# Seven products instead of eight for three pairs of groups in the first feed-forward layer, and sums and remainders of a pair's weights as operations of 2048 columns

## The chip, the cores and the metric

The kernel runs on one core of one Trainium2 chip. The metric is device time in microseconds (us) of one launch. Of the kernel before, three timed runs gave a median of 937.63 us (936.35 to 939.73); one further execution was recorded by the profiler, and every duration below comes from that one.

Five engines work side by side, each through its own list of instructions in order: PE (matrix products into PSUM), DVE (element by element), ACT (functions and copies), POOL (here a few small operations), SP (issues the loads). They wait for each other through semaphores.

## The reference, cut to what matters

The trunk has two layers on 256 tokens of 1024 features. Each layer adds half a SwiGLU feed-forward net, then a mixer (attention and pooling in layer 0, a state-space layer in layer 1), then another half SwiGLU net. So there are four nets, numbered f = 0 to 3 here, each with its own weights and D_FF = 2816.

```python
def _swiglu(h, w_gate, w_up, w_down):
    return (jax.nn.silu(h @ w_gate) * (h @ w_up)) @ w_down

x = x + 0.5 * _swiglu(_rmsnorm(x, ffn_norm[layer, 0]), ffn_w_gate[layer, 0], ...)
```

All is float32. Net 0 is the first work of the kernel: it runs while the machine starts up.

## The kernel before, in words

**Products in float32.** Each operand of a matrix product is split into a high part and a remainder, both in a reduced float32 type, and a product is three matmuls: high by high, remainder of the weights by high, high by remainder of the activations. ACT makes the high part (`wh`, L184), DVE the remainder (`wl`, L141 as `tt`). The activations h, transposed, lie in `hTh` and `hTl`.

**Groups.** D_FF is cut into NG = 11 groups of 256 columns, numbered 0 to 10. A group's gate and up weights are two units (`f` units, halves of the 1024 rows; 4096 columns of a partition together), its down weights one unit (2048 columns). PE computes gate and up for both halves of the tokens (t = 0, 1): 4 blocks of 12 matmuls of 512 columns into PSUM tiles `wk`; ACT applies silu (`sg`), DVE multiplies (`pr`); PE transposes the result (`sk<-ident,pr`), ACT and DVE split it (`hh`, `hl`); then 24 matmuls of the *previous or same* group's down projection into the accumulators `acc`. `ffn_joint` writes that order.

**Pairs.** In net f = 3 three pairs of groups, beginning at 2, 5 and 8 (PAIRS, L43), use another formula: the gate/up product of two groups is a 2 by 2 block product (two halves of the 1024 input features by two groups, two halves of the tokens), and in Strassen's form, as Winograd wrote it, it takes 7 block products instead of 8, each of 12 matmuls of 512 columns (`pair_product`, j = 1 to 7, in the order 1, previous down, 6, 2, 7, 5, 4, 3). For that it needs sums of weights: `split_pair` makes them on DVE, three for j = 6 and one for j = 7, then splits each operand (`m` units; their raw data are the `sr` tiles, four of 1 MB). It also needs sums of activations (`pair_rows`, on DVE) and their transposes `sTh`, `sTl` (`pair_turn`, four times four transposes on PE, put behind the blocks of group 1). The sums of products are made by DVE (one by ACT) out of PSUM into tiles `u`: `u1` from j = 6, `u0` from j = 2 and so on; `u0` to `u3` feed `gate`, whose product is named `pp`. Two `wk` tiles exist, so the product after next can start only when the sums have read a `wk` tile.

**Order.** A list of steps is written out (`S(...)`). Before each step `pump` issues loads and splits ahead as far as the ring of split buffers (RING = 4 units) and of raw buffers (RAW = 4 pieces of 512 KB) allow. Each engine's list follows from these steps with priorities; PE, DVE and ACT keep their order at run time. A buffer of the split ring becomes free when PE has finished the product four units earlier; so the copy for j = 4 waits for the end of product 6, and that for j = 3 for the end of product 2.

**Net 0** starts with `first`, `second`, `third` (loading and transposing x), then groups 0 to 10 jointly. After group 3 `opened` loads the mixer's constants and issues the rotary tables, some sixty small operations on DVE, in between. `tail` ends it.

Of the kernel before, what the change touches and what calls it, by code (L numbers as in the profile page):

```python
# [42 lines left out]
PAIRS = {3: (2, 5, 8)}  # L43
# [69 lines left out]
def trunk_kernel(ctx: ExitStack, tc: tile.TileContext, I, out):  # L113
# [199 lines left out]
    def split_pair(u):  # L313

        _, f, g, j = u
        b11, b21, b12, b22 = (raws.get((f, g, n, kh)) for n in range(2) for kh in range(2))
        h, l = (wsp.tile([128, 4, 2, 256], F32R, tag=tg, name=tg) for tg in ("wh", "wl"))
        lf = pr_["t2"]
        parts = [slice(0, 2), slice(2, 4)]
        with behind("split"):  # L320
            if j == 6:
                for k in parts:
                    tt(b11[:, k], b12[:, k], b11[:, k], ALU.subtract)
                    tt(lf[:, k], b11[:, k], b22[:, k], ALU.subtract)
                    tt(b21[:, k], b21[:, k], lf[:, k], ALU.add)
            if j == 7:
                for k in parts:
                    tt(b12[:, k], b22[:, k], b12[:, k], ALU.subtract)
            r = {1: b11, 2: b21, 3: b22, 4: b21, 5: b11, 6: lf, 7: b12}[j]
            for k in parts:  # L330
                keep("splits", hi_of(h[:, k], r[:, k]), tt(l[:, k], r[:, k], h[:, k].bitcast(F32), ALU.subtract))
        held[u] = (h, l)
# [122 lines left out]
    def gate_up(f, g, t, kh, ks):  # L455
# [3 lines left out]
        if (f, g, t) not in gups:  # L459
            gups[f, g, t] = wk((128, 2, 256))  # L460
# [32 lines left out]
    def pair_rows(f):  # L493

        a11, a12, a21, a22 = (hn[t][:, c * 512:(c + 1) * 512] for t in range(2) for c in range(2))
        rho = pr_["rho"]
        if f == 0:
            gv = pr_["pool"].tile([128, DM], F32, name="pg")
            SP.dma_start(out=gv, in_=I["ffn_norm"][0, 0].partition_broadcast(128))
            for t in range(2):  # L500
                for c in range(2):
                    o = slice(c * 512, (c + 1) * 512)
                    tt(hn[t][:, o], xs[t][:, o], gv[:, o], ALU.mult)
        root = pr_["pool"].tile([128, 1], F32, name="root")
# [56 lines left out]
    def hid_T(f, g, *ts):  # L561
# [6 lines left out]
        ps = sk((128, 2, len(ts) * 128))  # L568
# [22 lines left out]
    def even_open():  # L591
        at["pool"] = p = tc.alloc_tile_pool(name="even", bufs=1)
# [6 lines left out]
        at["psc"] = p.tile([128, 4], F32, name="psc")  # L599
# [5 lines left out]
        SP.dma_start(out=at["pos"], in_=I["positions"][0].rearrange("(t p) -> p t", p=128))  # L605
        at["qk"] = [p.tile([128, 2, 8, 64], F32, name=f"qk{t}") for t in range(2)]
# [16 lines left out]
        at["cs"] = p.tile([128, 2, 2, 2, 8], F32, name="cs")  # L623
# [94 lines left out]
    def rotary_tables():  # L718
        p = at["pool"]
# [699 lines left out]
    def ffn_joint(f, g0, g1):  # L1419

        for g in range(g0, g1):
            paced.add(len(steps))
            for kh in range(2):
                if f == 1 and g == NG - 1 and kh:
                    S(hold)
                for t in range(2):
# [3 lines left out]
                    if g == 1 and f in PAIRS:  # L1430
                        S(lambda n=2 * kh + t: pair_turn(n))
# [5 lines left out]
    def ffn_pairs(f, g0, g1):  # L1437

        g = g0
        while g < g1:  # L1440
# [10 lines left out]
            HID(f, g, 0, 1)  # L1451
            dn(f, g, 0)
# [60 lines left out]
    def first():  # L1513
        row = hn[1][0:8, 0:128]
# [60 lines left out]
    ffn_joint(0, 1, 4)  # L1575

    def opened():
        with behind("load"):
            load_g("m0", I["mix_norm"][0])
            even_open()  # L1580
        rotary_tables()
    S(opened)
    ffn_joint(0, 4, NG)
# [43 lines left out]
    S(lambda: at["pool"].release())  # L1627
# [147 lines left out]
```

## Time and profile before

| | |
|---|---|
| median of 3 runs | 937.63 us (936.35 to 939.73) |
| profiled execution | 937.66 us, span 935.9 us |
| PE busy | 914.7 us (98%) |
| DVE busy | 711.3 us (76%) |
| ACT busy | 464.9 us (50%) |
| loads and stores | 184.59 MB, mean 197 GB/s |

The span runs from the first to the last instruction recorded; the profiled execution's own time is 1.76 us longer. A row of a timeline gives start, duration, engine, line of the program, operation and operands; "x4" is four instructions merged, so the distance of two starts, not the duration, is what a block costs. In brackets stands the idle time before and what ended it. Net 0 takes the span's first 199 us, net 3 the last 175 us.

### The profile page before, as it was taken

What the parts mean: (1) busy time and instruction counts of PE and PEld (TensorE: products, weight loads), DVE (VectorE), ACT (ScalarE), POOL (GpSimd) and SP (SyncE); (2) the same over time, 40 slices, a digit from 0 to 9 for tenths busy, and PEclk for the clock granted to TensorE, in tenths of its full rate; (3) what the DMA queues carried; (4) which work ended last, traced back from release to release, by engine and by line L of the source; (5) the groups of instructions that cost most, each with busy time, mean ns of one, the idle gap of its engine ahead of it and who ended that gap; (6) DMA issues with size and microseconds to landing.
All of it is one profiled execution on the core that took longest, in us unless ns stands there. A gap on an engine that the chain in (4) does not pass through costs nothing.

```text
span 935.9 us, 13253 instructions
## 1 busy us (share of the span) xinstructions
PE 914.7 (98%) x4981; PEld 755.9 (81%) x4981; DVE 711.3 (76%) x1141; ACT 464.9 (50%) x643; POOL 64.9 (7%) x114
## 2 busy tenths in 40 slices
PE   7999999999999999999999999999879999999998
PEld 5888888889988888888888888888658788887876
DVE  5756654578967659999896557999496689999992
ACT  6544444455536444434454444444345465656561
POOL 0000000013020000000132001600200000000000
PEclk9999999999999999999999999999999999999999
DMA  7867656654476877556788655865956941939141
GB/s 249 276 193 219 192 183 200 193 166 142 134 193 202 197 228 209 174 154 209 235 240 295 191 180 165 250 206 183 301 217 194 333 148 47 335 101 320 53 134 46
DMA packets 149055, 184.59 MB, mean 197 GB/s; under 512 B 23160, under 2 KB 131648, under 8 KB 148224
## 3 DMA queue, kind: packets, MB, share of 16 engines
q1 hardware_dynamic: 145184, 174.70, 60.0%
q0 software_dynamic: 3504, 8.92, 3.8%
q8 instruction: 39, 0.64, 0.3%
q10 hardware_dynamic: 304, 0.14, 0.1%
q14 instruction: 24, 0.20, 0.1%
HBM read 173.24 MB, written 9.44 MB: 195 GB/s over the span
## 4 chain that ended last, share of the span: by engine, by line
PE 76%; DVE 9%; DMA 7%; ACT 3%; issue 3%; POOL 1%; SPq 0%; ACTq 0%; DVEq 0%; POOLq 0%
PE wk L103 46%; PE acc L103 25%; PE sk L103 5%; DMA raw<-in_ffn_w_up_dram 3%; DVE wl L141 3%; DMA raw<-in_s_w_glu_dram 2%; ACT wh L184 1%; DMA V<-x 1%; DVE X L141 1%; DVE b_t L141 1%; POOL r L742 1%; DMA raw<-in_ffn_w_gate_dram 1%; ACT acc L383 0%; ACT h L1211 0%; DVE b_q L141 0%
## 5 line engine op out<-in xcount | busy, mean ns | idle before, releaser
L141 DVE TENSOR_TENSOR wl<-raw,wh 128x1024 fp32r<-128x1024 f32 (+1 forms) x281 | 335.1, 1217 | 119.6 <-ACT wh L184 118.7
L184 ACT ACTIVATE wh<-raw 128x1024 fp32r<-128x1024 f32 (+1 forms) x281 | 285.6, 1051 | 216.0 <-PE wk L103 94.5
L103 PE MATMUL wk<-wh,hTh 128*128 128x512 f32 (+1 forms) x776 | 203.1, 380 | 3.0 <-DVE pr L150 1.5
L103 PE MATMUL wk<-wl,hTh 128*128 128x512 f32 (+1 forms) x776 | 200.2, 377 | 0.0
L103 PE MATMUL wk<-wh,hTl 128*128 128x512 f32 (+1 forms) x776 | 199.4, 376 | 0.0
L103 PEld LDWEIGHTS wk<-wh,hTh 128*128 128x128 f32 x776 | 139.6, 189 | 30.2 <-ACT hTh L184 2.5
L103 PEld LDWEIGHTS wk<-wl,hTh 128*128 128x128 f32 x776 | 140.8, 189 | 26.5 <-DVE wl L141 0.2
L103 PEld LDWEIGHTS wk<-wh,hTl 128*128 128x128 f32 x776 | 140.8, 189 | 26.4
L103 PE MATMUL acc<-wh,hh 128*128 128x512 f32 x352 | 141.4, 402 | 1.4 <-ACT hh L184 1.4
L103 PE MATMUL acc<-wl,hh 128*128 128x512 f32 x352 | 137.2, 390 | 0.0
L103 PE MATMUL acc<-wh,hl 128*128 128x512 f32 x352 | 137.0, 392 | 0.0
L478 ACT ACTIVATE sg<-wk,rstd 128x256 f32<-128x256 f32 x76 | 35.8, 472 | 95.1 <-PE wk L103 90.5
L103 PEld LDWEIGHTS acc<-wh,hh 128*128 128x128 f32 x352 | 66.2, 188 | 14.8 <-ACT hh L184 2.7
L103 PEld LDWEIGHTS acc<-wh,hl 128*128 128x128 f32 x352 | 66.1, 188 | 14.8 <-DVE hl L141 0.7
L103 PEld LDWEIGHTS acc<-wl,hh 128*128 128x128 f32 x352 | 66.3, 188 | 12.4
L150 DVE SCALAR_TENSOR_TENSOR pr<-wk,rstd,sg 128x256 f32<-128x256 f32 x76 | 36.4, 480 | 35.9 <-ACT sg L478 35.9
L141 DVE TENSOR_TENSOR wl<-sr,wh 128x1024 fp32r<-128x1024 f32 x36 | 42.8, 1219 | 2.6 <-ACT wh L184 2.6
L184 ACT ACTIVATE hh<-sk 128x512 fp32r<-128x512 f32 (+1 forms) x52 | 27.4, 527 | 29.6 <-PE sk L103 29.6
L184 ACT ACTIVATE wh<-sr 128x1024 fp32r<-128x1024 f32 x36 | 36.2, 1052 | 11.5 <-PE acc L103 5.2
L141 DVE TENSOR_TENSOR hl<-sk,hh 128x512 fp32r<-128x512 f32 (+1 forms) x52 | 31.3, 604 | 4.3 <-ACT hh L184 4.3
L383 ACT ACTIVATE acc<-x 128x512 f32<-128x512 f32 x24 | 14.3, 597 | 22.6 <-DVE x L150 18.3
L103 PE MATMUL sk<-ident,pr 128*128 128x128 f32 x152 | 24.4, 273 | 0.3 <-DVE pr L150 0.3
(322 smaller groups left out, 819.7 us busy)
## 6 DMA issues: line engine op xcount, KB each, us to landing
raw<-in_ffn_w_down_dram SPq DMA_DIRECT2D x88, 512.0 KB
raw<-in_ffn_w_up_dram SPq DMA_DIRECT2D x76, 512.0 KB
raw<-in_ffn_w_gate_dram SPq DMA_DIRECT2D x75, 512.0 KB
raw<-in_ev_w_in_dram SPq DMA_DIRECT2D x16, 512.0 KB
raw<-in_s_w_glu_dram SPq DMA_DIRECT2D x16, 512.0 KB
sr<-in_ffn_w_gate_dram SPq DMA_DIRECT2D x12, 512.0 KB
sr<-in_ffn_w_up_dram SPq DMA_DIRECT2D x12, 512.0 KB
raw<-in_ev_w_out_dram SPq DMA_DIRECT2D x8, 512.0 KB
```

The lines of the kernel that those rows point to most:

```text
L103: i = f(*a, **k)
L141: return DVE.tensor_tensor(out=o, in0=a, in1=b, op=op)
L150: return DVE.scalar_tensor_tensor(out=o, in0=a, scalar=s, in1=b, op0=op0, op1=op1)
L184: return ACT.activation(out=o, in_=i, func=AF.Copy)
L383: keep("square", ACT.activation(out=into or acc_of(t)[c], in_=xs[t][:, s], func=AF.Square, scale=1.0 / 32.0, accum_out=sums[t][:, c:c + 1]))
L478: ACT.activation(out=sg, in_=ps[:, 0], func=AF.Silu, scale=rstds[f, t])
L742: POOL.tensor_tensor(out=r8, in0=s8, in1=mhalf.to_broadcast([128, 8]), op=ALU.pow)
```

## The change

Net 0 gets three pairs too, beginning at groups 3, 6 and 9, so groups 3 to 10 without 5 and 8 go two by two. With it come the same side works as in net 3: the transposes `pair_turn` (behind the blocks of group 2, since the first pair begins at 3), `pair_rows`, which in net 0 also multiplies x by the norm's gains, loaded once more across all partitions (0.5 MB). The pool of the pair's tiles is open from the start, so the mixer's big tiles are allocated after net 0, its constants before. Group 1's gate and up blocks write to `sk` tiles, group 0's transposes to `wk` tiles. The rotary tables are issued after the first pair. The last pair ends net 0, directly before `tail`.

In both nets the sums and the remainders of `m` units are one operation of 2048 columns where they were two of 1024; the high copies on ACT stay two of 1024.

```diff
-PAIRS = {3: (2, 5, 8)}
+PAIRS = {0: (3,6,9,), 3: (2,5,8,)}
...
         lf = pr_["t2"]
-        parts = [slice(0, 2), slice(2, 4)]
         with behind("split"):
             if j == 6:
-                for k in parts:
-                    tt(b11[:, k], b12[:, k], b11[:, k], ALU.subtract)
-                    tt(lf[:, k], b11[:, k], b22[:, k], ALU.subtract)
-                    tt(b21[:, k], b21[:, k], lf[:, k], ALU.add)
+                tt(b11, b12, b11, ALU.subtract)
+                tt(lf, b11, b22, ALU.subtract)
+                tt(b21, b21, lf, ALU.add)
             if j == 7:
-                for k in parts:
-                    tt(b12[:, k], b22[:, k], b12[:, k], ALU.subtract)
+                tt(b12, b22, b12, ALU.subtract)
             r = {1: b11, 2: b21, 3: b22, 4: b21, 5: b11, 6: lf, 7: b12}[j]
-            for k in parts:
-                keep("splits", hi_of(h[:, k], r[:, k]), tt(l[:, k], r[:, k], h[:, k].bitcast(F32), ALU.subtract))
+            for k in (slice(0, 2), slice(2, 4)):
+                i = hi_of(h[:, k], r[:, k])
+            keep("splits", i, tt(l, r, h.bitcast(F32), ALU.subtract))
...
-            gups[f, g, t] = wk((128, 2, 256))
+
+            gups[f, g, t] = (sk if (f, g) == (0, 1) else wk)((128, 2, 256))
...
         if f == 0:
-            gv = pr_["pool"].tile([128, DM], F32, name="pg")
+            gv = tmp.tile([128, DM], F32, tag="gvec", name="gvec", bufs=1)
             SP.dma_start(out=gv, in_=I["ffn_norm"][0, 0].partition_broadcast(128))
...
-        ps = sk((128, 2, len(ts) * 128))
+        ps = (wk if (f, g) == (0, 0) else sk)((128, 2, len(ts) * 128))
...
-                    if g == 1 and f in PAIRS:
+                    if f in PAIRS and g == PAIRS[f][0] - 1:
                         S(lambda n=2 * kh + t: pair_turn(n))
...
             HID(f, g, 0, 1)
+            if g == NG - 2:
+                return
             dn(f, g, 0)
...
     def first():
+        at["pre"] = tc.alloc_tile_pool(name="even_pre", bufs=1)
+        pair_open(0)
...
-    ffn_joint(0, 1, 4)
+    S(lambda: pair_rows(0))
+    ffn_pairs(0, 1, 5)
 
     def opened():
         with behind("load"):
             load_g("m0", I["mix_norm"][0])
-            even_open()
+            even_load()
         rotary_tables()
     S(opened)
-    ffn_joint(0, 4, NG)
+    ffn_pairs(0, 5, NG)
+    S(lambda: pr_["pool"].release())
+    S(even_open)
     tail(0, N(0, "m0"), HT(0))
```

Three places show what moves. The first is DVE at the start of net 0, from the mean squares (`ss`) to the first `pr` of group 0. Before:

```order
L150 SCALAR_TENSOR_TENSOR ss<-ss 128x1 x2
L141 TENSOR_TENSOR wl<-raw,wh 128x4x256
L150 SCALAR_TENSOR_TENSOR pr<-wk,rstd,sg 128x256
L141 TENSOR_TENSOR wl<-raw,wh 128x4x256
L150 SCALAR_TENSOR_TENSOR pr<-wk,rstd,sg 128x256
```

and now:

```order
L150 SCALAR_TENSOR_TENSOR ss<-ss 128x1 x2
L141 TENSOR_TENSOR prho<-rstd,root 128x1
L141 TENSOR_TENSOR prho<-prho,root 128x1
L141 TENSOR_TENSOR h_85<-x_81,gvec 128x512
L141 TENSOR_TENSOR wl<-raw,wh 128x4x256
L150 SCALAR_TENSOR_TENSOR pr<-wk,rstd,sg 128x256 x2
```

The ratio of the two halves' norms (`prho`, from POOL's `root`) and the first of the four multiplications by the gains now stand ahead of the remainder of the second half of group 1's first unit.

The second place is DVE in the first pair of net 3, from the remainder of j = 6 (`wl<-t`) on; `u_6844` (now `u_6932`) is `u0`, the tile of product 2, `u_6845` (`u_6933`) is `u1`, that of product 6. Before:

```order
L141 TENSOR_TENSOR wl<-t_6848,wh 128x1024
L141 TENSOR_TENSOR sr<-sr 128x1024
L141 TENSOR_TENSOR wl<-sr,wh 128x1024 x2
L141 TENSOR_TENSOR u_6845<-wk,u_6844 128x512
L141 TENSOR_TENSOR wl<-sr,wh 128x1024 x2
L150 SCALAR_TENSOR_TENSOR u_6844<-wk,prho,u_6844 128x512
L141 TENSOR_TENSOR wl<-sr,wh 128x1024 x2
L150 SCALAR_TENSOR_TENSOR pp<-u_6844,rstd,sg 128x256
L141 TENSOR_TENSOR u_6846<-wk,u_6845 128x512
```

and now:

```order
L141 TENSOR_TENSOR wl<-t_6936,wh 128x2048
L141 TENSOR_TENSOR wl<-sr,wh 128x2048 x2
L141 TENSOR_TENSOR u_6933<-wk,u_6932 128x512
L141 TENSOR_TENSOR wl<-sr,wh 128x2048
L150 SCALAR_TENSOR_TENSOR u_6932<-wk,prho,u_6932 128x512
L141 TENSOR_TENSOR u_6934<-wk,u_6933 128x512
L141 TENSOR_TENSOR wl<-sr,wh 128x2048
L150 SCALAR_TENSOR_TENSOR pp<-u_6932,rstd,sg 128x256
```

After `u1` stood the remainder of j = 5 and then `u0`; now j = 5 is done ahead of `u1`, and the one between `u1` and `u0` is that of j = 4. The second pair of net 0 has the same order, with rotary operations in between:

```order
L141 TENSOR_TENSOR wl<-sr,wh 128x2048
L141 TENSOR_TENSOR u_96<-wk,u_95 128x512
L150 SCALAR_TENSOR_TENSOR rtr<-rtq,rtr 128x16
L145 TENSOR_SCALAR rto<-rto 128x16
L141 TENSOR_TENSOR wl<-sr,wh 128x2048
L150 SCALAR_TENSOR_TENSOR u_95<-wk,prho,u_95 128x512
L141 TENSOR_TENSOR u_97<-wk,u_96 128x512
```

Here `u_96` is `u1` and `u_95` is `u0`. In pairs 1 and 3 of net 0 and pairs 2 and 3 of net 3 `u0` stands ahead of the remainder of j = 4.

The third place is PE at the end of the last pair of net 0; the first three rows are product 3:

```order
L103 MATMUL wk<-wh,sTh 128x512 x4
L103 MATMUL wk<-wl,sTh 128x512 x4
L103 MATMUL wk<-wh,sTl 128x512 x4
L103 MATMUL sk<-ident,pp 128x128 x2
L103 MATMUL acc_414<-wh,hh 128x512
L103 MATMUL acc_414<-wl,hh 128x512
```

No other product stands between the transposes of `pp` and the first matmul that reads their split `hh`. At the end of the first pair four matmuls of the next group do:

```order
L103 MATMUL sk<-ident,pp 128x128 x2
L103 MATMUL wk<-wh,hTh 128x512 x4
L103 MATMUL acc_414<-wh,hh 128x512
```

## Rows read from the trace of the kernel before

**Rows 1.** The page, part 1: busy time of each engine, share of span.

```profile
PE 914.7 (98%) x4981; PEld 755.9 (81%) x4981; DVE 711.3 (76%) x1141; ACT 464.9 (50%) x643; POOL 64.9 (7%) x114
```

**Rows 2.** The page, part 4: the chain of waits, by engine.

```profile
PE 76%; DVE 9%; DMA 7%; ACT 3%; issue 3%; POOL 1%; SPq 0%; ACTq 0%; DVEq 0%; POOLq 0%
```

**Rows 3.** Net 0 by stretches: length, busy (count) per engine, clock, DMA share, GB/s.

```profile
57.64:74.43 16.79, 16.79 (x78) 13.90 (x76) 8.63 (x9) 7.46 (x9) 0.00 (x0) 1.00 0.62 186
...
74.43:91.21 16.78, 16.78 (x77) 13.90 (x76) 10.07 (x23) 7.46 (x9) 0.00 (x0) 1.00 0.78 245
...
91.21:108.00 16.79, 16.79 (x77) 13.90 (x76) 13.80 (x53) 7.46 (x9) 0.00 (x0) 1.00 0.66 197
...
0.00:60.00 60.00, 55.08 (x249) 44.00 (x250) 37.02 (x46) 36.01 (x51) 1.89 (x13) 1.00 0.78 247
...
25.00:45.00 20.00, 20.00 (x94) 16.44 (x93) 14.92 (x16) 11.47 (x15) 0.00 (x0) 1.00 0.89 281
```

**Rows 4.** Timeline of PE, net 0, blocks of gate and up of group 2.

```profile
40.85 1.07 PE L103 MATMUL wk<-wh,hTh 128*128 128x512 f32 x4
41.76 1.07 PE L103 MATMUL wk<-wl,hTh 128*128 128x512 f32 x4
```

**Rows 5.** Net 3 by stretches: two periods of a pair and a joint group.

```profile
781.01:829.20 48.19, 47.97 (x217) 39.34 (x216) 46.75 (x50) 29.04 (x34) 0.00 (x0) 1.00 0.60 197
829.20:877.47 48.27, 48.01 (x217) 39.26 (x216) 47.34 (x51) 29.38 (x34) 0.00 (x0) 1.00 0.61 196
```

**Rows 6.** Timeline of PE, net 3: transposes of a turn, the blocks behind them.

```profile
764.81 0.60 PE L103 MATMUL sk<-ident,h 128*128 128x128 f32 x4
765.16 1.17 PE L103 MATMUL wk<-wh,hTh 128*128 128x512 f32 x4
766.17 1.07 PE L103 MATMUL wk<-wl,hTh 128*128 128x512 f32 x4
```

**Rows 7.** Timeline of PE, net 3: ends of pairs 1 and 3.

```profile
806.65 0.38 PE L103 MATMUL sk<-ident,pp 128*128 128x128 f32 x2
...
807.72 0.50 PE L103 MATMUL acc<-wh,hh 128*128 128x512 f32 x1 [0.22 <-ACT hh L184]
...
905.81 0.51 PE L103 MATMUL acc<-wh,hh 128*128 128x512 f32 x1 [0.88 <-ACT hh L184]
```

**Rows 8.** Timeline of ACT, net 3: `hh` at the end of pair 1.

```profile
807.07 0.60 ACT L184 ACTIVATE hh<-sk 128x512 fp32r<-128x512 f32 x1 [1.89 <-PE sk L103]
```

**Rows 9.** Timeline of PE, net 3: products 2, 5 (pair 1), 5 (pair 2).

```profile
791.89 1.07 PE L103 MATMUL wk<-wh,hTh 128*128 128x512 f32 x4
...
797.33 1.07 PE L103 MATMUL wk<-wh,sTh 128*128 128x512 f32 x4
...
845.52 0.84 PE L103 MATMUL wk<-wh,sTh 128*128 128x512 f32 x3
```

**Rows 10.** Timeline of DVE, net 3: sums and remainders in pairs 1 and 2.

```profile
792.09 0.69 DVE L141 TENSOR_TENSOR u<-wk,u 128x512 f32<-128x512 f32 x1 [0.17 <-PE wk L103]
792.70 2.35 DVE L141 TENSOR_TENSOR wl<-sr,wh 128x1024 fp32r<-128x1024 f32 x2
794.97 0.75 DVE L150 SCALAR_TENSOR_TENSOR u<-wk,prho,u 128x512 f32<-128x512 f32 x1
...
843.86 0.74 DVE L150 SCALAR_TENSOR_TENSOR u<-wk,prho,u 128x512 f32<-128x512 f32 x1
```

**Rows 11.** The page, part 5: ACT, high copies of pairs.

```profile
L184 ACT ACTIVATE wh<-sr 128x1024 fp32r<-128x1024 f32 x36 | 36.2, 1052 | 11.5 <-PE acc L103 5.2
```

**Rows 12.** Timelines of PE and DVE at the start of net 0.

```profile
23.37 1.21 PE L103 MATMUL wk<-wh,hTh 128*128 128x512 f32 x4 [1.47 <-DVE pr L150]
...
24.42 1.09 PE L103 MATMUL wk<-wl,hTh 128*128 128x512 f32 x4
...
20.74 0.16 DVE L150 SCALAR_TENSOR_TENSOR ss<-ss 128x1 f32<-128x1 f32 x1 [1.29 <-ACT acc L383]
...
21.69 1.23 DVE L141 TENSOR_TENSOR wl<-raw,wh 128x1024 fp32r<-128x1024 f32 x1 [0.79 <-ACT wh L184]
```

More of the change, by code (lines that the diff above doesn't have):

```diff
@@ L589, in trunk_kernel, with even_load @@
     at = {}
-    def even_open():
-        at["pool"] = p = tc.alloc_tile_pool(name="even", bufs=1)
+    def even_load():
+        p = at["pre"]
         for nm, c0, n in (("NA", C_NA, 128), ("NB", C_NB, 256),
@@ L598, in even_open @@
         SP.dma_start(out=at["pw"], in_=I["ev_pool_w"][0].rearrange("g c e -> c g e"))
-        at["psc"] = p.tile([128, 4], F32, name="psc")
+        at["psc"] = p.tile([128, 52], F32, name="psc")[:, 0:4]
         SP.dma_start(out=at["psc"], in_=I["ev_pool_scale"][0].rearrange("(g e) -> e g", e=128))
@@ L605, in even_open @@
         SP.dma_start(out=at["pos"], in_=I["positions"][0].rearrange("(t p) -> p t", p=128))
+        at["cs"] = p.tile([128, 2, 2, 2, 8], F32, name="cs")
+    def even_open():
+        at["pool"] = p = tc.alloc_tile_pool(name="even", bufs=1)
         at["qk"] = [p.tile([128, 2, 8, 64], F32, name=f"qk{t}") for t in range(2)]
@@ L622, in even_open @@
         at["plT"] = [p.tile([128, 4, 128], F32, name=f"plT{t}") for t in range(2)]
-        at["cs"] = p.tile([128, 2, 2, 2, 8], F32, name="cs")
         at["ra"] = p.tile([128, 8, 2, 8], F32, name="ra")
@@ L718, in rotary_tables @@
     def rotary_tables():
-        p = at["pool"]
+        p = at["pre"]
         posf = p.tile([128, 2], F32, name="posf")
@@ L1626, in trunk_kernel @@
     C(table, AF.Silu)
-    S(lambda: at["pool"].release())
+    S(lambda: (at["pool"].release(), at["pre"].release()))
     S(s5_open)
```

## The prediction

> **What bounds the kernel now.** I read the page first. PE is busy 914.7 of 935.9 us, DVE 76% of the span, ACT half of it [rows 1]; in the chain of waits PE holds 76%, DVE 9%, the loads 7% [rows 2]. So a matmul less is time less, unless something that hides behind PE comes to light. The reader should then leave the averages for the stretches that change. A joint group of net 0 lasts 16.79 us with PE busy all of it and DVE 8.63 us, about half; where the rotary tables fall DVE has 10.07 and 13.80 [rows 3]. Net 3 already shows what a pair is like: one pair and one joint group last 48.19 and 48.27 us, with DVE busy 46.75 and 47.34 of them [rows 5]. There DVE is at 97 and 98%, and whatever is put on it there is near the end of its slack.
>
> **The products removed.** Four matmuls of a block take 41.76 - 40.85 = 0.907 us [rows 4], one 0.2267. A pair does 7 blocks of products where two groups do 8 at 12 matmuls: 3 pairs × 12 × 0.2267 = 8.16 us less on PE.
>
> **What a pair gives of this.** In net 3 a pair and a joint group last 48.19 or 48.27 us against 3 × 16.79 = 50.37: a gain of 2.18 and 2.10, not 2.72 [rows 3, 5]. The 0.6 us between goes into small matmuls and the wait for `hh` (0.22 us at the end of pair 1) [rows 7]. So pair 1 of net 0: -2.1.
>
> Pair 2 of net 0 differs by two things. The first is the place of `u0`. Take its twin, pair 1 of net 3. Product 6 ends where `u1` starts, at 792.09 [rows 10]. The copies for j = 4 may start then; two of them take 2 × 1.05 us [rows 11], to 794.2. The wide remainder needs both. Two remainders of 1024 take 794.97 - 792.70 = 2.27, one 1.135; 512 columns take 0.61 [rows 10]. So a column costs 1.03 ns and an operation 0.08 beside its columns, and one of 2048 about 2.2: 796.4. Then `u0`, 0.75: 797.2. Product 5, which wants the `wk` tile that `u0` reads, starts at 797.33 [rows 9]. Before, `u0` started at 794.97 and had 1.6 us to spare; in pair 2 of net 3 it started at 843.86 and had 0.9 [rows 9, 10]. Now it is 0.1 or 0.2. The second thing is the rotary tables: 58 instructions and 1.44 + 5.17 = 6.61 us of DVE more in the two stretches that hold them, 0.114 each [rows 3]. By the order 12 of them stand ahead of `u0` in pair 2 from the sums on, 1.4 us. Against that, 9 mergers ahead of it save 0.08 each, 0.7. If DVE has 0.1 of slack there, `u0` is late by 0.6; if the joint group ahead lets DVE run ahead, by nothing; if the mergers save nothing, 1.3. I take 0.55, between: pair 2 gives -1.55 (-2.1 to -0.7).
>
> Pair 3 has no joint group behind it. In net 3 the split `hh` starts 0.42 and PE goes on 1.07 us after the start of the last transposes of `pp` (806.65, 807.07, 807.72) [rows 7, 8]; two transposes take half of the 0.35 of four [rows 6], and other matmuls cover the rest but for 0.22. At the end of net 0 none do: 0.9 us, as at the end of pair 3 of net 3, where PE was idle 0.88 [rows 7]. I take 2.72 - 0.85: -1.87 (-2.7 to -1.6). The transposes of group 10 stand behind eleven `acc` matmuls, 2.5 us, in which DVE and ACT make their `pp` (0.6 for the sum and about as much each for silu and product): nothing.
>
> **What is added.** Four turns of four transposes in group 2: each takes 0.35 us until the next block starts, and that block's first quarter lasts 1.01 instead of 0.907 [rows 6], so 0.44 each, +1.76. They stand behind blocks that run back to back, so nothing hides them.
>
> The start. PE waits 1.47 us at 23.37 for `pr` to free a `wk` tile [rows 12]; with group 1 in `sk` this wait goes. Next late is the remainder that the second matmul block wants. It ended at 22.9 (21.69 + 1.23) [rows 12]; now two small operations and one of 512 columns stand ahead, and the first waits for POOL's `root`, which follows the last `ss` (20.74) by two operations of POOL. I put its end at 24.2 to 24.4, and in the trace PE reached that block at 24.42 [rows 12]. So the wait changes its cause and I take 0 (-1.4 to +0.5, if the gains' load is late). Behind it in DVE's queue are the two `pr` of group 0, which feed transposes that PE has behind group 1's first block. The other three multiplications and three operations of `pair_rows` take 6 × 0.61 = 3.7 us of DVE before the turns; DVE is busy 14.92 of 20 us from 25 to 45 [rows 3], so they fit, but they may shift the `pr` of group 1 and its transposes: +0.25 (0 to 1.5).
>
> The wide operations in net 3. Eleven mergers a pair save 0.9 us of DVE by the above, off PE's path except for the waits of 0.2 to 0.9 at the ends of pairs, which follow ACT. Pair 1 there gets the late `u0` described above. I take 0 (-0.7 to +1.4).
>
> The mixer's tiles are allocated after net 0 instead of inside it; only small loads of constants move, and they are not used before the mixer: nothing (0 to +0.3).
>
> **The sum.** -2.1 - 1.55 - 1.87 + 1.76 + 0.25 = -3.51 us, against the profiled execution of 937.66 us: 934.15. The median of the runs is 937.63, the same within 0.03, so I predict **934.2 us**.
>
> **Rivals.**
>
> *A, slower: the evacuations queue behind the wide operations everywhere.* A wide remainder starts only when both copies are there, 1.05 us later than its first half could, and DVE keeps its order: what stands behind it (`u0`, `u1`, `pp`) is late by as much, and PE waits for a `wk` tile. In a period of 48.2 us DVE has 48.19 - 46.75 = 1.4 us left [rows 5], plus 0.9 from the mergers. If two remainders of a pair wait so, 2.1 us, the slack of 0.9 at `u0` [rows 9, 10] is passed by 1.2 a pair. For six pairs that is 7.2 us on the forecast's sum, which already has 0.55 of them: 934.2 + 6.6 = 940.8. It decides from the point where DVE's idle time in a pair that ACT's copies end exceeds 0.9 us. For it: 97% of DVE. Against it: in pair 2 of net 3 `u0` already stood behind the remainder of j = 4, with 0.9 to spare. The Trainium skill speaks for it (Perfetto Trace Analysis, Optimizing Scalar/DVE Operations): if the Scalar or Vector engine isn't saturated but causes bubbles on others, breaking instructions up may let work be done sooner; the change does the opposite. The same section says that grouping helps a saturated engine; the trace has DVE saturated in pairs and not over the kernel, so by the page it could go either way. Chance 0.15.
>
> *B, no change: net 0 can't feed its pairs.* Two mechanisms with one price. First the loads: before the sums of pair 1 are done, some 8.8 us ahead of product 6 at about 67 us, x (1 MB), three groups' gate and up (6), three downs (3), the pair's four tiles (4) and the gains (0.5) must have come, 14.5 MB by about 58 us. The first 60 us moved them at 247 GB/s, 25 to 45 us at 281 [rows 3]; 14.5 MB at 247 take 58.7 us. Late by 1 to 3. Second DVE: a period with rotary operations would want 46.75 - 0.9 + 6.6 = 52.5 us of DVE in 48.2 [rows 3, 5]; as the tables spread over two periods, 2 × 45.9 + 6.6 = 98.4 in 96.4, 2.0 too much, less what the ring has in hand. Either costs about 3: 937.2. Against it: the ring is four units deep and groups 1, 2 and 5 leave DVE free. Chance 0.27.
>
> *C, more: the mergers bring DVE ahead.* Of the PSUM wait of 1.47 at the start 1.2 goes for good, pair 2 gives 2.1 and the waits of net 3 shrink by half of 0.22 + 0.88: -3.5 - 1.2 - 0.55 - 0.5 = -5.8, 931.9. Chance 0.13.
>
> **How the numbers follow.** Forecast 0.45 (own range 932.8 to 935.8), A 0.15, B 0.27, C 0.13. A measurement tells about 0.3% or 2.8 us from no change: 934.8 and 940.5. Faster: 0.36 of the forecast's 0.45, all of C, a little of B: 0.51. Slower: 0.09 of A and a little of B: 0.12. Between: 0.37. The range leaves out most of A, and the deep end of C: 931.8 to 938.9.
>
> **What would show it.** PE has 36 matmuls of 512 columns fewer in net 0 and 16 transposes more. Pairs 1 and 2 of net 0 with their joint group should last 48.2 and 48.8 us, where three groups lasted 50.4; group 2 with its turns 1.76 more than 16.79. At the end of pair 3 PE should be idle 0.8 to 0.9 <- ACT `hh`. The wait of 1.47 <- `pr` should be one of about the same length <- DVE `wl`. In pair 1 of net 3 `u0` should end within 0.3 us of the start of product 5. I am wrong if PE waits in net 0's pairs for `u` (A), for `wl` or a load (B), or if net 3 changes by more than a microsecond.

## The result, and the profile after

The changed kernel took 946.43 us (median of 6 runs, 944.36 to 949.70), the kernel before 938.73 (6 runs, 936.35 to 942.93): a ratio of 1.0078 (95% interval 1.0052 to 1.0104). Slower by 7.7 us, where 934.2 was predicted. The profiled execution took 947.15 us, with a span of 945.3, against 937.66 and 935.9.

The page of the changed kernel, parts 1 and 4, to be held against [rows 1, 2]:

```profile
PE 913.6 (97%) x4961; PEld 751.2 (79%) x4961; DVE 771.4 (82%) x1152; ACT 486.4 (51%) x668; POOL 65.0 (7%) x115
...
PE 58%; DVE 20%; DMA 10%; issue 6%; ACT 4%; SPq 1%; POOL 0%; ACTq 0%; DVEq 0%
```

PE has 20 instructions fewer, as foreseen (36 removed, 16 added), and is busy only 1.1 us less; DVE has 60 us more work. In the chain of waits DVE's share has doubled, from 9 to 20%.

The table cuts both profiled executions at the same work: the difference of each stretch, in us.

| stretch | before | after | difference | predicted |
|---|---|---|---|---|
| start to pair 3 (158.37; after 158.44) | 158.37 | 158.44 | +0.07 | -1.64 |
| pair 3 to the start of net 1 (284.11; 289.43) | 125.74 | 130.99 | +5.25 | -1.87 |
| nets 1 and 2 (to `sk<-by,sel` on PE) | 383.31 | 385.27 | +1.96 | 0 |
| state-space mixer (to the first matmuls of net 3) | 78.05 | 81.59 | +3.54 | 0 |
| net 3 (to the span's end) | 190.43 | 189.01 | -1.42 | 0 |

With 0.09 us outside the span this is the 9.49 us between the two executions. "Start of net 1" is PE's first transpose of its normalised input; all shifts below are of that mark, against 284.11 us.

Windows of the changed kernel in net 0 and the mixer behind it (columns as in [rows 3]): group 2 with its turns; pair 1 with group 5; pair 2 with group 8; pair 3 to the last `acc` matmul; the gap to the mixer; its first matmuls; the rest to its first `qk` transposes.

```profile
41.28:60.00 18.72, 18.72 (x94) 15.49 (x92) 16.12 (x15) 11.11 (x15) 0.00 (x0) 1.00 0.97 335
60.00:108.95 48.95, 48.42 (x217) 39.04 (x216) 44.58 (x43) 28.69 (x34) 0.00 (x0) 1.00 0.67 209
108.95:158.44 49.49, 48.86 (x218) 39.12 (x216) 48.10 (x82) 28.91 (x34) 0.00 (x0) 1.00 0.64 199
158.44:197.61 39.17, 37.54 (x165) 29.60 (x163) 36.86 (x45) 24.03 (x31) 0.57 (x6) 1.00 0.25 81
197.61:200.82 3.21, 1.42 (x9) 0.84 (x9) 2.27 (x5) 2.21 (x5) 0.27 (x1) 0.98 0.90 282
200.82:204.29 3.47, 3.47 (x17) 3.47 (x17) 3.47 (x5) 2.93 (x5) 0.92 (x1) 0.52 0.26 80
204.29:223.48 19.19, 16.44 (x138) 16.26 (x137) 15.55 (x28) 6.86 (x11) 4.70 (x3) 1.00 0.61 200
```

The same work in the kernel before, from group 9 to the mixer's `qk`:

```profile
158.37:199.21 40.84, 40.32 (x185) 32.90 (x184) 23.11 (x28) 20.07 (x28) 0.55 (x1) 1.00 0.55 173
...
199.21:217.65 18.44, 18.44 (x154) 18.18 (x152) 16.51 (x30) 9.78 (x17) 6.16 (x3) 1.00 0.64 203
```

DVE's column is the one to read. From group 9 to `qk` it rose from 39.6 to 58.2 us of work, in 59.3 and 65.0 us. PE did less (37.54 + 1.42 against 40.32), but the mixer's first stretch took 22.66 us instead of 18.44: 2.75 us idle, and the granted clock, after the gap in which PE was busy 1.42 of 3.21 us, at 0.52, so at the lower of its two levels (1.2 of 2.4 GHz), where it had been 1.00.

PE's largest waits there, in the changed kernel:

```profile
186.09 0.50 PE L103 MATMUL acc<-wh,hh 128*128 128x512 f32 x1 [0.69 <-ACT hh L184]
...
198.81 1.29 PE L103 MATMUL sk<-ident,h 128*128 128x128 f32 x8 [1.04 <-DVE h L150]
...
211.90 0.71 PE L103 MATMUL wk<-wh,hTh 128*128 128x256 f32 x4 [2.75 <-DVE qk L141]
```

And what DVE did ahead of that `h`. Before:

```profile
191.66 0.69 DVE L150 SCALAR_TENSOR_TENSOR x<-acc,x 128x512 f32<-128x512 f32 x1 [0.95 <-PE acc L103]
192.59 0.69 DVE L150 SCALAR_TENSOR_TENSOR x<-acc,x 128x512 f32<-128x512 f32 x1 [0.24 <-PE acc L103]
194.07 0.16 DVE L150 SCALAR_TENSOR_TENSOR ss<-ss 128x1 f32<-128x1 f32 x1 [0.79 <-ACT acc L383]
194.89 1.42 DVE L150 SCALAR_TENSOR_TENSOR h<-x,rstd,gvec 128x512 f32<-128x512 f32 x2 [0.66 <-POOL rstd L420]
```

and after:

```profile
192.09 0.68 DVE L150 SCALAR_TENSOR_TENSOR x<-acc,x 128x512 f32<-128x512 f32 x1
192.69 1.21 DVE L141 TENSOR_TENSOR wl<-raw,wh 128x1024 fp32r<-128x1024 f32 x1
193.82 0.68 DVE L150 SCALAR_TENSOR_TENSOR x<-acc,x 128x512 f32<-128x512 f32 x1
194.42 1.21 DVE L141 TENSOR_TENSOR wl<-raw,wh 128x1024 fp32r<-128x1024 f32 x1
195.96 1.23 DVE L141 TENSOR_TENSOR wl<-raw,wh 128x1024 fp32r<-128x1024 f32 x1 [0.32 <-ACT wh L184]
197.10 0.15 DVE L150 SCALAR_TENSOR_TENSOR ss<-ss 128x1 f32<-128x1 f32 x1
197.17 0.68 DVE L150 SCALAR_TENSOR_TENSOR x<-acc,x 128x512 f32<-128x512 f32 x1
197.92 1.41 DVE L150 SCALAR_TENSOR_TENSOR h<-x,rstd,gvec 128x512 f32<-128x512 f32 x2
```

Before, DVE has gaps and each small operation of the norm follows its cause. After, remainders of the mixer's weights that once fitted into group 10's slack stand between them, and the largest gap left is 0.32 us.

### The profile page after: what moved, and what is told of

Read it like the earlier page. It is cut to its first block, busy times and chain, and to the rows that moved or that the text cites. A ratio compares the mean times of both kernels' runs of the same rounds, so it can differ in the third digit from the quotient of the medians.

```text
span 945.3 us, 13218 instructions
## 1 busy us (share of the span) xinstructions
PE 913.6 (97%) x4961; PEld 751.2 (79%) x4961; DVE 771.4 (82%) x1152; ACT 486.4 (51%) x668; POOL 65.0 (7%) x115
## 3 DMA queue, kind: packets, MB, share of 16 engines
q1 hardware_dynamic: 145328, 175.22, 59.3%
## 4 chain that ended last, share of the span: by engine, by line
PE 58%; DVE 20%; DMA 10%; issue 6%; ACT 4%; SPq 1%; POOL 0%; ACTq 0%; DVEq 0%
PE wk L103 36%; PE acc L103 17%; DVE wl L141 8%; PE sk L103 5%; DMA raw<-in_ffn_w_up_dram 4%; ACT wh L184 2%; DVE X L141 2%; DMA raw<-in_s_w_glu_dram 1%; DMA raw<-in_ffn_w_down_dram 1%; DMA sr<-in_ffn_w_up_dram 1%; DVE u L141 1%; DVE sr L141 1%; DVE b_q L141 1%; DMA raw<-in_ev_w_in_dram 1%; DMA gvec<-in_ffn_norm_dram 1%
## 5 line engine op out<-in xcount | busy, mean ns | idle before, releaser
L141 DVE TENSOR_TENSOR wl<-raw,wh 128x1024 fp32r<-128x1024 f32 (+1 forms) x257 | 307.8, 1214 | 73.8 <-ACT wh L184 73.0
L184 ACT ACTIVATE wh<-raw 128x1024 fp32r<-128x1024 f32 (+1 forms) x257 | 263.5, 1052 | 191.8 <-PE wk L103 57.0
L103 PE MATMUL wk<-wh,hTh 128*128 128x512 f32 (+1 forms) x700 | 184.5, 382 | 5.3 <-DVE qk L141 2.8
L103 PE MATMUL wk<-wl,hTh 128*128 128x512 f32 (+1 forms) x700 | 180.6, 377 | 0.0
L103 PE MATMUL wk<-wh,hTl 128*128 128x512 f32 (+1 forms) x700 | 179.8, 376 | 0.7 <-DVE hTl L141 0.7
L103 PEld LDWEIGHTS wk<-wh,hTl 128*128 128x128 f32 x700 | 127.2, 190 | 24.5 <-DVE hTl L141 1.2
L141 DVE TENSOR_TENSOR wl<-sr,wh 128x2048 fp32r<-128x2048 f32 x36 | 82.1, 2283 | 8.2 <-ACT wh L184 8.2
L184 ACT ACTIVATE wh<-sr 128x1024 fp32r<-128x1024 f32 x72 | 71.6, 1050 | 27.4 <-DVE sr L141 12.1
L103 PE MATMUL wk<-wh,sTh 128*128 128x512 f32 x96 | 26.6, 399 | 1.6 <-DVE u L141 0.9
L141 DVE TENSOR_TENSOR sr<-sr 128x2048 f32<-128x2048 f32 x12 | 27.4, 2282 | 0.0
```

The source lines that it names most:

```text
L103: i = f(*a, **k)
L141: return DVE.tensor_tensor(out=o, in0=a, in1=b, op=op)
L184: return ACT.activation(out=o, in_=i, func=AF.Copy)
```

## The experiments

Theory D, formed on that: the last pair leaves DVE with a debt of remainders, and the debt falls due in the DVE-bound chain x, `ss`, `h`, `hTl`, `qk`. Rivals: PE's order at the end; the order of DVE's list; the wide operations; the pairs' own order (E); late loads (L); and for the state-space mixer, whether its 3.5 us belong to the change at all. All runs in one table, ratios against the kernel before timed beside them; the start of net 1 is read from one profiled execution each.

| run | time us | ratio (interval) | start of net 1 |
|---|---|---|---|
| e1 | 938.97 | 0.9985 (0.9962 to 1.0008) | +0.43 |
| e2 | 946.17 | 1.0053 (1.0032 to 1.0073) | +4.52 |
| e3 | 941.86 | 1.0006 (0.9985 to 1.0026) | +0.69 |
| e4 | 946.92 | 1.0063 (1.0039 to 1.0087) | +5.56 |
| e5 | 951.39 | 1.0101 (1.0080 to 1.0121) | +11.46 |
| e6 | 947.09 | 1.0060 (1.0040 to 1.0080) | +5.03 |
| e7 | 958.19 | 1.0189 (1.0167 to 1.0211) | +15.18 |
| e8 | 941.89 | one run | +1.51 |
| e9 | 939.39 | 1.0002 (0.9981 to 1.0023) | +0.24 |
| e10 | 959.28 | 1.0205 (1.0170 to 1.0241) | +16.19 |
| e11 | 976.58 | 1.0389 (1.0345 to 1.0433) | +30.77 |
| e12 | 941.47 | one run | +2.26 |
| e13 | 948.18 | one run | +8.07 |
| e14 | 939.09 | 0.9984 (0.9966 to 1.0003) | +0.28 |
| e15 | 941.13 | one run | +0.24 |
| e16 | 939.63 | 0.9995 (0.9975 to 1.0014) | -0.01 |
| e17 | 946.89 | 1.0071 (1.0047 to 1.0095) | +6.73 |
| e18 | 943.13 | one run | +1.84 |

**Which part of the change.** e1 is the kernel before with the wide operations alone (the hunk of `split_pair` in the diff above), e2 the changed kernel with that hunk undone. e3 leaves the third pair out:

```diff
-PAIRS = {0: (3,6,9,), 3: (2,5,8,)}
+PAIRS = {0: (3, 6), 3: (2,5,8,)}
```

> The kernel before, with only the sums and remainders of net 3's pairs as operations of 2048 columns; net 0 has no pairs. Theory T (the changed kernel loses at the end of net 0 and behind it, the wide operations are not to blame; in its net 3 the waits of 0.2 to 0.9 us at the ends of pairs are gone): 1.0 to 1.5 us faster than before, 0.9985 to 0.999 of its time. Rival W (the evacuations queue behind the wide operations): 1 to 3 us slower than before.

> The changed kernel, with the sums and remainders of pairs as two operations of 1024 columns again, in both nets; net 0 keeps its three pairs. T: the end of net 0 is as bad as in the changed kernel and DVE has 0.9 us more per pair, so 946 to 949 us, 1.009 to 1.012 of before. W: the loss goes, 939 to 941 us.

> The changed kernel without its last pair in net 0: groups 9 and 10 are joint again and the end of net 0 is that of before; wide operations stay. T: pairs 1 and 2 gained 1.42 and 0.88 us and the turns and the start cost 2.4, so net 0 comes out even, and the end's losses (about 2.4 of waits, 1.5 of low clock, 2.8 in the mixer) go: 937 to 939 us if the later losses (2 us in nets 1 and 2, 3.6 before the state-space layer) follow from them, 941 to 943 if those are of their own. W: 943 to 945.

The width is not the cause: without it the start of net 1 is nearly as late (+4.52; e2's ratio came out under the 1.009 that was expected). e1's gain of 1.0 to 1.5 us isn't shown, its interval reaches past 1. Two pairs cost 0.7 us at the start of net 1; the third costs 4.6 more. So two pairs with their turns about break even, and the loss belongs to the pair that ends the net.

**PE's order, and holding the splits.** e4 keeps PE's written order at the end of net 0 too (`S(strict(f <= 1))` in `tail`); e5 lets no further split be issued from product 4 of the last pair to the norm:

```diff
+                if f == 0 and g == NG - 2 and j == 4:
+                    S(hold)
...
+        if f == 0:
+            S(lambda: release("norm"))
```

> The changed kernel, with PE's order at the end of net 0 kept as the steps are written, so that the eight transposes of h stand ahead of the last six matmuls into acc instead of behind all of them. T: PE's idle time of 1.8 us and the low clock after it (1.5) shrink and the mixer starts 2 to 4 us earlier, 941 to 944 us. W, or any theory by which the end's order doesn't matter: 946.

> The changed kernel; from product 4 of net 0's last pair on no further weights are split until the norm's products h of the first half of the tokens are made, so that DVE does the end's short chain (x, ss, h) ahead of the mixer's remainders. Theory D (the last pair leaves DVE with a debt of remainders that falls due in the chain that ends net 0): the mixer starts 1 to 3 us earlier than in the changed kernel and its wait of 2.75 us for qk shrinks; net 1 starts 2 to 5 us earlier; 942 to 944 us. Rival O (the order at the end doesn't matter, since the mixer waits for DVE's sum of work in any case): net 1 starts within 1 us of the changed kernel; 946.

e4, expected at 941 to 944 us, missed: it moved the wait (2.74 us at the transposes of `h`, none at `qk`) and kept the sum. e5 missed too: the norm was hardly earlier, and the mixer's first `qk` transposes came 6 us later than in the changed kernel. DVE in e5:

```profile
192.58 1.31 DVE L150 SCALAR_TENSOR_TENSOR x<-acc,x 128x512 f32<-128x512 f32 x2
196.61 0.16 DVE L150 SCALAR_TENSOR_TENSOR ss<-ss 128x1 f32<-128x1 f32 x1 [2.73 <-ACT acc L381]
```

DVE stood idle for 2.73 us while the remainders waited, and PE then waited 5.51 us at `qk`. In ACT's queue the sums of squares stood behind a copy that waited 2.09 us for a load of the mixer's weights; that brought up L. Here, too, the debt was not paid by being put off.

DVE's list is a rival that the traces settle. Before, one of the first two `qk` stands ahead of the `hTl` of the second half of the tokens; in the changed kernel both stand behind it. Before:

```profile
205.37 0.42 DVE L141 TENSOR_TENSOR qk<-wk,gqk 128x256 f32<-128x256 f32 x1
205.70 1.28 DVE L141 TENSOR_TENSOR hTl<-sk,hTh 128x512 fp32r<-128x512 f32 x2
```

and after:

```profile
208.18 1.29 DVE L141 TENSOR_TENSOR hTl<-sk,hTh 128x512 fp32r<-128x512 f32 x2 [0.77 <-ACT hTh L184]
...
211.34 0.75 DVE L141 TENSOR_TENSOR qk<-wk,gqk 128x256 f32<-128x256 f32 x2
```

In e2 and e4 the list has the order of before again, PE waits there 0.59 us and not at all, and net 1 still starts at +4.52 and +5.56. So this order decides where PE waits, and hardly how much is lost.

**The third pair elsewhere.** e6 has pairs at 3, 6 and 8 (group 10 joint), e7 at 2, 5 and 8, by PAIRS alone.

> The changed kernel with net 0's pairs beginning at groups 3, 6 and 8, so that the pairs stay three and group 10 is joint: the end of net 0 has a joint group's DVE work (8.6 us in 16.8) ahead of it. D: net 1 starts 4 to 6 us earlier than in the changed kernel, at the time of before or up to 1.5 us earlier; 939 to 942 us. O, or pairs that cost as much as they save wherever they stand: net 1 starts 2 us later than before or more; 943 to 946.

> The changed kernel with net 0's pairs at 2, 5 and 8, as in net 3: a joint group after each pair and at the end, but the first pair 16.8 us earlier, when the loads run at 286 to 335 GB/s. D: the end is like before's; net 1 starts up to 3 us earlier than before if the loads keep up (937 to 940 us), 2 to 5 us later if the first pair waits for its weights. O: 943 to 946.

D's 939 to 942 us for e6 were missed. Its end is clean (mixer +5.00, start of net 1 +5.03), but the 5 us are lost earlier, behind the two adjacent pairs:

```profile
134.00:183.00 49.00, 44.92 (x191) 34.28 (x190) 47.22 (x75) 23.79 (x30) 0.29 (x5) 0.97 0.29 87
```

DVE is busy for 96% of it; ACT's copies wait 4.13 and 5.10 us for DVE's sums, and PE for `wh` and `wl`. That looks like the same debt, due at once; no run tried it apart. e7 shows rival B's first half, the loads at the start. DVE waits for one load of the pair's weights; that sum, two more and the operations that make `h` stand behind it, and PE waits 14.46 us for the transposes of `h`:

```profile
36.81 2.29 DVE L141 TENSOR_TENSOR sr<-sr 128x2048 f32<-128x2048 f32 x1 [4.52 <-DMA sr<-in_ffn_w_up_dram]
...
48.02 1.11 PE L103 MATMUL sk<-ident,h 128*128 128x128 f32 x4 [14.46 <-DVE h L150]
```

**Taking DVE's sums away.** e8 leaves the last pair's four sums out, e12 those of all three pairs of net 0 (both then multiply other weights and serve for their times alone, as do e17 and e18); e10 and e11 give the same sums to GpSimd (`POOL.tensor_tensor`).

```diff
-            if j == 6:
+            if j == 6 and (f, g) != (0, 9):
...
-            if j == 7:
+            if j == 7 and (f, g) != (0, 9):
...
```

> The changed kernel, but the last pair of net 0 leaves out its four sums of weights (it multiplies the weights as they come), 8.8 us of DVE less just ahead of the end. D: the waits of the end go, the mixer's wait for qk is under 0.5 us, and net 1 starts 4 to 6 us earlier than in the changed kernel. O, or a cause in PE's order alone: net 1 starts within 1.5 us of the changed kernel.

> The changed kernel with all sums of weights in the three pairs of the first network left out (products 2, 4, 5, 6 and 7 then take plain weights, so the output is not the reference's). It frees 3 x 9.2 us of VectorE and takes no TensorE work away. Theory D (VectorE's work in the pairs eats what the 36 matmuls save): the three pairs give nearly their 3 x 2.78 us less the 1.9 us of the turns, so the second network starts at -3 to -1 us and the time is 935 to 938 us. Rival E (the pairs lose time by their own order, in the chains of product, u, sg, pp, hh, whatever VectorE has beside it): the second network starts at +1 to +2 us as without the last pair's sums alone, the time is 940 to 942 us.

> The changed kernel with the four sums of weights of the last pair of the first network done by GpSimd, which is idle there, instead of VectorE. Theory D (VectorE's debt at the end of the first network is the loss; leaving out these sums altogether brought the start of the second network from +5.3 to +1.5 us against before): if GpSimd does a sum of 128x2048 in under 6 us each, that start comes at +1.5 to +2.5 us and the time at 941.5 to 943.5 us. Rival P (GpSimd takes over 6 us for a sum, or slows VectorE's own operations beside it): TensorE waits at products 6 and 7 of the pair, the start of the second network stays at +5 us or later and the time at 946 us or more.

> The changed kernel with the sums of weights of all three pairs of the first network on GpSimd. Theory D with a GpSimd sum of under 6 us: the other two pairs lose their waits at u, pp and hh too (some 1.2 us of gaps in the trace), so the second network starts at 0 to +1.5 us and the time is 939.5 to 942.5 us. Rival P: each pair waits for its sums, the second network starts 3 times as late as with the last pair alone, the time is 950 us or more.

Without the last pair's sums, 9 us of DVE, net 1 starts 3.8 us earlier (+5.32 to +1.51; D had expected 4 to 6), and the wait at `qk` is gone. The three runs without these sums (e8, e12, e18) took 941.5 to 943.1 us, all under the fastest of seven runs of the changed kernel, 944.36. Taking the other pairs' sums away as well gives nothing more (+2.26): D's -3 to -1 was wrong there, and E's forecast holds. What is left shows in e8 at the pair's own end:

```profile
184.56 0.44 PE L103 MATMUL sk<-ident,pp 128*128 128x128 f32 x2 [1.25 <-DVE pp L150]
185.69 0.50 PE L103 MATMUL acc<-wh,hh 128*128 128x512 f32 x1 [0.69 <-ACT hh L184]
...
197.28 0.63 PE L103 MATMUL sk<-ident,h 128*128 128x128 f32 x4 [1.50 <-DVE h L150]
```

GpSimd is no way out. In e10 its sums and DVE beside them, and what PE waited for:

```profile
149.33 5.61 POOL L322 TENSOR_TENSOR sr<-sr 128x2048 f32<-128x2048 f32 x1 [126.78 <-DVE rtu L145]
...
160.45 4.50 POOL L326 TENSOR_TENSOR sr<-sr 128x2048 f32<-128x2048 f32 x1
...
150.39 4.59 DVE L150 SCALAR_TENSOR_TENSOR rtu<-rtu,rtm 128x16 f32<-128x16 f32 x1
...
160.45 4.53 DVE L141 TENSOR_TENSOR rtm<-rtm,rto 128x16 f32<-128x16 f32 x1
...
166.79 0.69 PE L103 MATMUL sk<-ident,pr 128*128 128x128 f32 x2 [9.79 <-DVE pr L150]
```

GpSimd took 4.50 to 5.61 us for a sum, DVE takes 2.28. That is under the 6 us that both expectations named, so D's 941.5 to 943.5 us were due, and were missed. What came is the second half of rival P: GpSimd slows DVE. Three rotary operations of 16 columns, 0.17 us elsewhere, lasted 4.59, 4.10 and 4.53 us, each until the sum beside it ended (154.98 and 154.94 us for the first). `pr` of group 8 stood behind them, and PE waited 9.79 us for it, ahead of the last pair. With all pairs' sums on GpSimd (e11) net 1 starts 31 us late.

**Late loads.** In the changed kernel the loads of the mixer's weights are first issued at 184.32 us (172.15 before). e16 was to delay them in the kernel before; e17 loads half of each piece and uses it twice; e18 adds e8's edit.

```diff
-        for k in (slice(0, 2), slice(2, 4)) if i == 0 else (slice(None),):
+        for k in (slice(0, 2), slice(2, 4)) if i == 0 else (slice(0, 2) if kind == "i" else slice(None),):
...
+                    if units[i][0] == "i":
+                        hk, lk = (v[s].rearrange("p (a b) f -> p a (b f)", a=2) for v in (h, l))
+                        rk = r[:, 0:2].rearrange("p b f -> p (b f)").unsqueeze(1).to_broadcast([128, 2, 512])
```

> The kernel before, no pairs in the first network, but the loads of the mixer's input weights wait for the matmuls of the first half of the tokens of group 10, which end at about 183 us; in the profile of before the first was issued at 172.15 us, in that of the changed kernel at 184.32. Theory L (late loads): ACT's copies wait for loads, the norm's sums and the transposes behind them are late, the second network starts at +3 to +6 us and the time is 943 to 946 us. Theory D (VectorE's debt of sums and remainders): VectorE has no debt here, the loads are hidden by its slack, the second network starts at 0 to +1.5 us and the time stays within 1.5 us of before.

> The changed kernel with only half of each piece of the mixer's input weights loaded, each used twice by operations of the same sizes, so the output is not the reference's; 4 MB less to load, VectorE's work unchanged. Theory L: the waits of ACT for these loads go, the second network starts at +1 to +3 us instead of +5.3 and the time is 941 to 944 us. Theory D: it starts at +4.5 us or later, the time stays at 945 us or more.

> As e17, and the last pair of the first network leaves out its four sums of weights as well, so the output is not the reference's. Theory L: with the loads out of the way the sums matter little, the start of the second network is within 1 us of that of e17. Theory D: it is the sums that count, the start is that of the run without the sums alone, +1.5 us, well ahead of e17's.

e16 is no test: its loads were issued at 172.12 us, so the edit (`behind("late")`) delayed nothing, and it counts as one more execution of the kernel before. For the others the start of net 1 misleads, since e17 is late by 1.9 us ahead of the last pair already. The table counts from the start of that pair; its last row is the time that ACT's copies waited for these loads.

| us | before | changed (first, e13) | e17 | e18 | e8 | e12 |
|---|---|---|---|---|---|---|
| start of pair 3 | 158.37 | 158.44, 157.60 | 160.24 | 157.34 | 158.10 | 159.39 |
| pair 3 to net 1 | 125.74 | 130.99, 134.58 | 130.60 | 128.61 | 127.52 | 126.98 |
| ACT waiting for the loads | none | 4.0, 4.9 | 2.2 | 3.9 | 4.7 | 4.1 |

With the loads halved 4.9 of the 5.25 us are still lost, and DVE has no gap over 0.44 us up to `qk`. Without the sums ACT waits for loads as long as ever (e8, 4.7 us) and the stretch is 3.5 us shorter. So the loads are not the cause; DVE's work is. Loads can hurt all the same: in e18 a copy that waited 1.65 us for one stood ahead of `hh`, and PE waited 2.22 us for that. In e17:

```profile
196.36 1.22 DVE L141 TENSOR_TENSOR wl<-raw,wh 128x1024 fp32r<-128x1024 f32 x1
197.49 0.15 DVE L150 SCALAR_TENSOR_TENSOR ss<-ss 128x1 f32<-128x1 f32 x1
197.56 1.22 DVE L141 TENSOR_TENSOR wl<-raw,wh 128x1024 fp32r<-128x1024 f32 x1
...
212.03 1.20 PE L103 MATMUL wk<-wh,hTh 128*128 128x256 f32 x4 [3.40 <-DVE qk L141]
```

**What is not the change.** e9 and e15 are the kernel before again, e13 the changed one, e14 is e1 again.

> The kernel before once more, with no edit, to see how far two executions of one program lie apart. The profiled executions of all variants so far wait 3.8 to 5.7 us at the first transposes of the S5 layer for the gathered state V, the one of the kernel before 2.13 us. Theory V (the landing time of V differs from execution to execution): a wait of over 3 us here too, a span of 938 to 941 us, ratio 1.000 +- 0.002. Rival W (the wider operations of the third network or the pairs of the first cause it): a wait of 2.1 +- 0.4 us and a span of 936 us.

> The changed kernel once more, with no edit, one look. Theory V (the S5 layer's time differs from execution to execution, whatever the kernel): the stretch from the last matmuls of the third network to the first of the fourth takes 79.5 to 81 us here, under the 81.59 of its first profile, and the second network starts at +5.3 +- 0.4 us as before. Rival W (the changed kernel brings a longer S5 layer): 81.6 +- 0.4 us again.

> The kernel before with the wide sums and remainders in the pairs of the fourth network alone, as in e1, in five rounds. Theory: the fourth network is 1.4 to 1.8 us shorter and nothing else is changed, so the ratio is 0.9982 +- 0.0012, under 1 with its whole interval. Rival (the 1.8 us are given back in the S5 layer, whose wait for V was 3.78 us in e1): ratio 0.9995 to 1.0005.

> The kernel before a third time, with no edit, one look. Theory V: the stretch of the S5 layer takes 79 to 81 us, nearer to the 80.39 of e9 than to the 78.05 of the first profile. Rival W: 78.0 to 78.5 us, and e9 was the exception.

| stretch | kernel before (first, e9, e15, e16) | changed (first, e13) | wide alone (e1, e14) |
|---|---|---|---|
| nets 1 and 2 | 383.31, 382.64, 383.68, 382.79 | 385.27, 384.56 | 384.25, 383.12 |
| state-space mixer | 78.05, 80.39, 81.24, 80.22 | 81.59, 80.54 | 80.55, 80.53 |
| net 3 | 190.43, 189.02, 190.03, 189.99 | 189.01, 189.12 | 188.66, 189.16 |

The first profile of before was a fast one in the state-space mixer: PE's wait there for the gathered state was 2.13 us, and in e15, the same program, 4.94:

```profile
678.30 0.72 PE L103 MATMUL wk<-ident,h 128*128 128x128 f32 x2 [4.94 <-DVE h L141]
```

In e9 it was 2.63, where over 3 was expected, and the stretch still 2.3 us longer than in the first, so this wait is only part of the spread. On the means (79.98 and 81.07) 1.1 us remain, less than the spread, and stay open. Net 3 gains 0.8 to 1.0 on the means, not 1.4, and e9 of the kernel before, 189.02, is as short as the changed one. The 1.8 us of nets 1 and 2 (on the means) are outside the spread; in both executions of the changed kernel PE waits there 1.75 and 1.67 us, at the end of net 1, for `hl`, `h` and `hTl`, and DVE waits for the next norm's gains. In the kernel before neither happens:

```profile
478.26 1.29 DVE L141 TENSOR_TENSOR h<-x,gvec 128x512 f32<-128x512 f32 x2 [2.59 <-DMA gvec<-in_ffn_norm_dram]
```

That load was issued at 470.58 us, 7.7 ahead of its use (460.03 and 9.5 before). Why it stands later among the loads was not tried. e13 missed its own forecast for the start of net 1 (+5.3 +- 0.4; it was +8.07), and e14 its interval under 1.

## Why the prediction was wrong

**The step that failed** is pair 3 and what follows it: "The transposes of group 10 stand behind eleven `acc` matmuls ... nothing", and the mixer "nothing (0 to +0.3)". I priced the pair's end by PE's wait for `hh` (0.85; measured 0.69) and never followed DVE past the end of the pair. A pair and its joint group gave DVE work for 47 of 48 us in [rows 5]; behind pair 3 stands no joint group but a tail whose norm runs through DVE. The -1.87 became +5.25. From pair 3 to net 1 PE waited 6.66 us by its rows where it had waited 1.31; the half clock in the mixer cost 1.5 more; the remainder, fewer matmuls, gave back 1.6. Of the 5.25, 3.5 go with the pair's four sums (e8; held against e13 it is 7.1), the low clock among them, since e8 kept a clock of 1.00 from pair 3 to `qk`. The other 1.8, where -1.87 was forecast, are at the pair's own end (`pp` 1.25, `hh` 0.69, `h` 1.50 in e8), and no run took these apart. None of the rivals named this; B had DVE's shortage, but put it into the rotary stretch.

**Pairs 1 and 2** took 48.95 and 49.49 us instead of 48.2 and 48.8, so -1.42 and -0.88 for -2.1 and -1.55. In e13 they took 48.24 and 49.38: pair 1 is right within what two executions differ by (0.53 of waiting for `pp` in the first is not in e13), pair 2 was mis-sized, at the short end of its range. Pair 2 waits 0.59 at `u1`, ahead of product 7, behind rotary operations; that this is near the 0.55 that the prediction gave `u0` and product 5 is luck. By e12 DVE's sums are not what these two lack.

**The turns** took 18.72 - 16.79 = 1.93 (predicted 1.76; 0.35 + 0.10 from [rows 6] is 0.45 a turn, so 1.8). **The start**: the wait of 1.47 for `pr` became one for `wl`, as foreseen, and with group 1's work it cost 0.43 us (predicted 0.25). The row that answers to [rows 12]:

```profile
24.75 1.19 PE L103 MATMUL sk<-wl,hTh 128*128 128x512 f32 x4 [1.37 <-DVE wl L141]
```

**Net 3**, put at 0 (-0.7 to +1.4), took about 0.8 us less on the means, within the spread of the kernel before. The waits for `hh` of [rows 7] are gone in all four executions with wide operations; e9 of the kernel before has only the one of 0.22. The periods are hardly shorter (96.30 us for the two, 96.46 before); those of [rows 5] now read:

```profile
791.70:839.90 48.20, 48.20 (x218) 38.95 (x217) 46.27 (x38) 29.01 (x34) 0.00 (x0) 1.00 0.62 196
839.90:888.00 48.10, 48.09 (x219) 39.46 (x218) 43.97 (x37) 29.07 (x34) 0.00 (x0) 1.00 0.62 197
```

PE waits for nothing in them. Over the whole of net 3 DVE is busy 159.25 and 159.50 us in e1 and e14, 161.66 and 161.34 in the first execution of the kernel before and e9: the 33 mergers save about 2.1, near the 0.08 each that was worked out. In pair 1 there `u0` ends at 808.15 us, 0.15 ahead of product 5, as worked out:

```profile
807.41 0.74 DVE L150 SCALAR_TENSOR_TENSOR u<-wk,prho,u 128x512 f32<-128x512 f32 x1
...
808.30 1.17 PE L103 MATMUL wk<-wh,sTh 128*128 128x512 f32 x4
```

So in net 3 rival A did not come. In pair 3 of net 0 its sign did: DVE stood idle 1.35 us for ACT's copies ahead of a wide remainder, `u1` stood behind that, and PE waited for two tiles of `u`:

```profile
169.72 2.29 DVE L141 TENSOR_TENSOR wl<-sr,wh 128x2048 fp32r<-128x2048 f32 x1 [1.35 <-ACT wh L184]
...
172.75 1.16 PE L103 MATMUL wk<-wh,sTh 128*128 128x512 f32 x4 [0.56 <-DVE u L141]
...
182.21 1.16 PE L103 MATMUL wk<-wh,sTh 128*128 128x512 f32 x4 [0.39 <-DVE u L141]
```

With its 0.69 for `hh` the pair waits 1.64 us; with the width undone (e2) it waits 3.05, for `pp` and `hh`. So A named waits that came, but they are not the loss. The rule that was weighed for it is in a section that covers both ways (the Trainium skill, Perfetto Trace Analysis, Optimizing Scalar/DVE Operations). The traces here agree with its other half, that grouping helps a saturated engine, as far as DVE's 2.1 us go; a gain in time is not shown.

No variant beats the kernel before beyond its interval; the wide operations in net 3 alone come nearest, 0.9985 and 0.9984, each interval just reaching 1.

## What to carry to other kernels

Before trading matmuls for vector work, add up the vector engine's work over the stretch *behind* the trade, up to the next point where its own results are on the path; a busy share of 95% is free only while slack follows. In these runs a debt put off, moved to GpSimd or given better loads was still due, and the last block of the net was a bad place for it; two pairs next to each other were as bad. And profile the unchanged kernel more than once before reading a stretch of 3 us as an effect.

## What the hardware showed that was not expected

After the idle gap ahead of the mixer the granted clock fell to half and stayed there for 3.5 us in one execution. In e13 it stayed there until about 206.5 us, and after the wait of 2.75 us at `qk` it fell again (0.59 from 213.14 to 216.50 us), which the same wait did not bring in the first. The same matmuls kept PE busy 18.44 us before, 19.91 after and 22.62 in e13:

```profile
200.83:226.21 25.38, 22.62 (x153) 22.45 (x154) 19.03 (x32) 9.81 (x16) 5.62 (x3) 0.81 0.47 155
```

So PE's waits, 1.8 us ahead of the mixer in the first and 2.6 and 2.75 in e13, cost 1.5 and 4.2 us more behind them, and two executions of one program differ by that: +5.32 and +8.07. And a sum on GpSimd held up small operations of DVE until it ended, 4.1 to 4.6 us instead of 0.17 (e10).
